# A batched matrix product on one core: the first two batches of y are issued from ScalarE's DMA queue

## The chip, the core and the metric

The kernel runs on one core of a Trainium2 chip. A core has five engines that run their own instruction streams and wait for each other through semaphores: TensorE (PE in the profile, with its weight loads as PEld), VectorE (DVE), ScalarE (ACT), GpSimd (POOL) and SyncE (SP). Transfers between HBM and the on-chip memory SBUF are issued as instructions by one of these engines; the profile shows an issue as a row of the issuer's sequencer (SPq for SyncE) and the transfer itself as work of the core's 16 DMA engines. The metric is the device time of one execution in microseconds (us), and the kernel before and the changed one are compared by it.

## What is computed

Thirty-two independent matrix products in float32, each of a 256x512 matrix by a 512x384 one:

```python
batch, dim_i, dim_j, dim_k = 32, 256, 512, 384
x: (batch, dim_i, dim_j) float32     # 16.8 MB
y: (batch, dim_j, dim_k) float32     # 25.2 MB
np.einsum('bij,bjk->bik', x, y).astype(np.float32)   # 12.6 MB
```

The inputs are 41.94 MB and the output is 12.58 MB, the figures that the profile gives as read and written.

## The kernel before

x is loaded four batches at a time (`Q = 4`), in 8 transfers of 2048 KB. The 128 partitions hold 4 batches of 32 row groups; each partition takes 8 successive rows of x, 16 KB in one piece. y is loaded one batch per transfer (768 KB, 6 KB in one piece per partition), two batches to a tile (`G = 2`), so there are 16 steps, called units u below, and 32 transfers of y. The output of a unit is stored by one transfer of 768 KB, 16 in all. Every transfer is issued by SyncE, in the order in which the program writes them, because each is passed to `keep`, which fixes the order of instructions on their engine.

For every group of four batches, TensorE turns the rows of x over (L99, a transpose against an identity matrix, 32 per group in two halves), and VectorE and ScalarE take turns in copying the result out of PSUM as float16 (L105, L107). The y of a unit is cast to float16 by the two engines in turn (`round_y`, L116 on ScalarE and L118 on VectorE). `multiply(u)` then makes 32 matrix products (L130) into four PSUM tiles, `collect(u)` copies these to SBUF (L143 on ScalarE, L145 on VectorE), and `store(u)` issues the store (L150).

The loop of L160 is written as a software pipeline. At its step s it issues the loads of unit s + 2, collects unit s - 2, multiplies unit s - 1, casts the y of unit s, makes the transposes of the next group of x, and stores unit s - 2. Before the loop, units 0 and 1 are loaded. So SyncE's order begins with the first group of x (L66), the two batches of y of unit 0 (L81), the second group of x, two batches of unit 1 and two of unit 2; then the third group of x, and so on, with a store between the loads from step 2 on. A store that waits for `collect` holds up what is written behind it on SyncE.

The framework inserts all waits. The pools give three tiles to x, five to y, two each to the float16 copies, five to the output, and four PSUM tiles each to transposes and products. ScalarE's stream begins with the load of its function table, which needs no data; its first copy (L107) needs the fifth to eighth transposes.

Of the kernel before, what the change touches and what calls it, by code (L numbers as in the profile page):

```python
# [1 line left out]

# [5 lines left out]


MM_DT = mybir.dt.float16  # L10
F32 = mybir.dt.float32
P = 128


Q = 4
G = 2

LAG = 4


@with_exitstack
def kernel(
    ctx: ExitStack,
    tc: tile.TileContext,
    x: bass.AP,
    y: bass.AP,
    out: bass.AP,
):
    nc = tc.nc

    B, I, J = x.shape
    _, _, K = y.shape


    M = P // G
    NE = I // M
    NJ = J // P

    PQ = P // Q
    R = I // PQ
    H = R // NE
    U = B // G

    const_pool = ctx.enter_context(tc.tile_pool(name="const", bufs=1))
    x_pool = ctx.enter_context(tc.tile_pool(name="x_pool", bufs=3))
    y_pool = ctx.enter_context(tc.tile_pool(name="y_pool", bufs=5))
    yr_pool = ctx.enter_context(tc.tile_pool(name="yr_pool", bufs=2))
    xt_pool = ctx.enter_context(tc.tile_pool(name="xt_pool", bufs=2))  # L50
    o_pool = ctx.enter_context(tc.tile_pool(name="o_pool", bufs=5))
    tpsum_pool = ctx.enter_context(tc.tile_pool(name="tpsum", bufs=4, space=bass.MemoryType.PSUM))
    opsum_pool = ctx.enter_context(tc.tile_pool(name="opsum", bufs=4, space=bass.MemoryType.PSUM))


    keep = tc.keep_in_program_order

    identity = const_pool.tile([P, P], F32)
    make_identity(nc, identity)

    x_of, y_of, yr_of, xt_of, ps_of, o_of = {}, {}, {}, {}, {}, {}

    def load_x(q):
        x_of[q] = x_pool.tile([P, R, J], F32, name="x_sb")
        keep(
            nc.sync.dma_start(  # L66
                out=x_of[q],
                in_=x[q * Q : (q + 1) * Q].rearrange("g (p r) j -> (g p) r j", r=R),
            )
        )  # L70

    def load(u):

        if u == 0:
            load_x(0)
        if (u + 1) * G % Q == 0 and u + 1 < U:
            load_x((u + 1) * G // Q)
        y_of[u] = y_pool.tile([P, G, NJ, K], F32, name="y_sb")
        for g in range(G):
            keep(  # L80
                nc.sync.dma_start(  # L81
                    out=y_of[u][:, g],
                    in_=y[u * G + g].rearrange("(q t) k -> q t k", q=P),
                )
            )

    def transpose(q, half):

        x_sb = x_of[q]
        if half == 0:  # L90
            xt_of[q] = xt_pool.tile([P, NJ, NE, Q * PQ, H], MM_DT, name="xt_sb")
        n = 0
        for t in range(half * NJ // 2, (half + 1) * NJ // 2):
            for e in range(0, NE, 2):
                t_ps = tpsum_pool.tile([P, 2, H, Q * PQ], F32, name="t_ps")
                for f in range(2):
                    for h in range(H):
                        keep(
                            nc.tensor.transpose(  # L99
                                t_ps[:, f, h], x_sb[:, h * NE + e + f, t::NJ], identity  # L100
                            )
                        )
                dst = xt_of[q][:, t, e : e + 2].rearrange("c f p h -> c f h p")
                if n % 2 == 0:
                    keep(nc.vector.tensor_copy(dst, t_ps))  # L105
                else:
                    keep(nc.scalar.copy(dst, t_ps))  # L107
                n += 1

    def round_y(u):  # L110
        y_sb = y_of.pop(u)
        yr_of[u] = yr_pool.tile([P, G, NJ, K], MM_DT, name="y_r")
        for g in range(G):
            for t in range(NJ):
                if t % 2 == 0:
                    keep(nc.scalar.copy(yr_of[u][:, g, t], y_sb[:, g, t]))  # L116
                else:
                    keep(nc.vector.tensor_copy(yr_of[u][:, g, t], y_sb[:, g, t]))  # L118

    def multiply(u):  # L120
        xt_sb, y_r = xt_of[u * G // Q], yr_of.pop(u)
        ps_of[u] = []
        for e in range(NE):
            o_ps = opsum_pool.tile([P, K], F32, name="o_ps")
            ps_of[u].append(o_ps)
            for t in range(NJ):
                for g in range(G):
                    a = (u * G + g) % Q
                    keep(
                        nc.tensor.matmul(  # L130
                            o_ps[g * M : (g + 1) * M],
                            xt_sb[:, t, e, a * PQ : (a + 1) * PQ].rearrange("c p h -> c (p h)"),
                            y_r[:, g, t],
                            start=(t == 0),
                            stop=(t == NJ - 1),
                        )
                    )

    def collect(u):
        o_of[u] = o_pool.tile([P, NE, K], F32, name="o_sb")  # L140
        for e in range(NE):
            if e % 2 == 0:
                keep(nc.scalar.copy(o_of[u][:, e], ps_of[u][e]))  # L143
            else:
                keep(nc.vector.tensor_copy(o_of[u][:, e], ps_of[u][e]))  # L145
        del ps_of[u]

    def store(u):
        keep(
            nc.sync.dma_start(  # L150
                out=out[u * G : (u + 1) * G].rearrange("g (m e) k -> (g m) e k", e=NE),
                in_=o_of.pop(u),
            )
        )


    ahead = LAG - 2
    for u in range(ahead):
        load(u)
    for s in range(U + 2):  # L160
        if s + ahead < U:
            load(s + ahead)
        if s == 0:
            transpose(0, 0)
            transpose(0, 1)
        if s >= 2:
            collect(s - 2)
        if 1 <= s <= U:
            multiply(s - 1)
        if s < U:  # L170
            round_y(s)
        for half in range(2):
            q = (s + 1 - half) * G // Q
            if (s + 1 - half) * G % Q == 0 and 0 < q < B // Q:
                transpose(q, half)
        if s >= 2:
            store(s - 2)


# [1 line left out]
_INS = ['x', 'y']  # L181
_OUTS = [((32, 256, 384), 'float32')]


# [23 lines left out]
```

## Time and profile before

| what | value |
|---|---|
| median of 5 runs | 136.11 us (136.0 to 136.46) |
| the profiled execution | 136.0 us, of which the span of the profile is 134.1 us |
| TensorE busy | 89.6 us (67%) |
| VectorE, ScalarE busy | 56.2 us (42%), 63.9 us (48%) |
| the DMA queue's packets, as a share of 16 engines' span | 97.9% |
| transfers | 56, together 54.53 MB |
| mean rate over the span | 406 GB/s read and written |

The span runs from the first instruction to the last of the profiled execution; 1.9 us of the time lie outside it. The views used are the page (shares by engine, 40 slices, queues, the chain of work that ended last, groups of instructions), the instructions in order of time, the waits, and tables of short stretches. In a row of the order of time, the first number is the start in us from the span's start, the second the time to the end of the last instruction of the merged row, and brackets give the idle time before it and what ended it. In a table of stretches the columns are the stretch, its length, the busy time of PE, PEld, DVE, ACT and POOL with instruction counts, the granted TensorE clock, the share of the DMA engines' time, and GB/s; bytes count where their packet starts, so a share can pass 1.

### The profile page before, as it was taken

What the parts mean: (1) busy time and instruction counts of PE and PEld (TensorE: products, weight loads), DVE (VectorE), ACT (ScalarE), POOL (GpSimd) and SP (SyncE); (2) the same over time, 40 slices, a digit from 0 to 9 for tenths busy, and PEclk for the clock granted to TensorE, in tenths of its full rate; (3) what the DMA queues carried; (4) which work ended last, traced back from release to release, by engine and by line L of the source; (5) the groups of instructions that cost most, each with busy time, mean ns of one, the idle gap of its engine ahead of it and who ended that gap; (6) DMA issues with size and microseconds to landing.
All of it is one profiled execution on the core that took longest, in us unless ns stands there. A gap on an engine that the chain in (4) does not pass through costs nothing.

```text
span 134.1 us, 1968 instructions
## 1 busy us (share of the span) xinstructions
PE 89.6 (67%) x768; PEld 73.9 (55%) x768; DVE 56.2 (42%) x128; ACT 63.9 (48%) x129; POOL 0.7 (1%) x6
## 2 busy tenths in 40 slices
PE   0049494979189786886089780997839792597920
PEld 0049474868168665666068660776727682476810
DVE  0004617471652456611634418324273704628520
ACT  3004837661771467621754428424375605737710
POOL 2000000000000000000000000000000000000000
PEclk9999999999959999999968996579977999779998
DMA  5999999999999999999999999999999999999993
GB/s 107 415 398 462 398 431 412 450 404 410 416 451 415 408 425 423 452 398 421 415 448 431 403 421 421 451 423 399 423 425 453 406 412 420 427 421 423 419 394 164
DMA packets 8074, 54.65 MB, mean 407 GB/s; under 512 B 897, under 2 KB 897, under 8 KB 7041
## 3 DMA queue, kind: packets, MB, share of 16 engines
q1 hardware_dynamic: 8064, 54.53, 97.9%
q8 instruction: 6, 0.10, 0.3%
q14 instruction: 4, 0.02, 0.0%
HBM read 41.94 MB, written 12.58 MB: 406 GB/s over the span
## 4 chain that ended last, share of the span: by engine, by line
DMA 78%; PE 13%; ACT 4%; DVE 0%; issue 0%
DMA y_sb<-in_y_dram 40%; DMA x_sb<-in_x_dram 38%; PE o_ps L130 9%; PE t_ps L99 3%; ACT xt_sb L107 2%; ACT y_r L116 1%; ACT o_sb L143 1%; DVE o_sb L145 0%
## 5 line engine op out<-in xcount | busy, mean ns | idle before, releaser
L130 PE MATMUL o_ps<-y_r,xt_sb 128*64 128x384 f16 x512 | 53.6, 370 | 28.9 <-ACT o_sb L143 21.1
L130 PEld LDWEIGHTS <-xt_sb 128*64 128x64 f16 x512 | 39.9, 124 | 39.7 <-issue 22.8
L116 ACT CAST y_r<-y_sb 128x384 f16<-128x384 f32 x64 | 29.5, 513 | 37.7 <-DMA y_sb<-in_y_dram 37.6
L99 PE MATMUL t_ps<-identity,x_sb 128*128 128x128 f32 x256 | 36.8, 301 | 10.0 <-DMA x_sb<-in_x_dram 9.9
L99 PEld LDWEIGHTS t_ps<-identity,x_sb 128*128 128x128 f32 x256 | 34.0, 211 | 14.5 <-issue 14.1
L118 DVE CAST y_r<-y_sb 128x384 f16<-128x384 f32 x64 | 20.0, 356 | 45.6 <-DMA y_sb<-in_y_dram 45.6
L107 ACT CAST xt_sb<-t_ps 128x512 f16<-128x512 f32 x32 | 22.5, 731 | 24.7 <-PE t_ps L99 24.6
L105 DVE CAST xt_sb<-t_ps 128x512 f16<-128x512 f32 x32 | 22.5, 728 | 25.0 <-PE t_ps L99 24.9
L145 DVE COPY o_sb<-o_ps 128x384 f32<-128x384 f32 x32 | 16.3, 545 | 2.1 <-PE o_ps L130 2.1
L143 ACT COPY o_sb<-o_ps 128x384 f32<-128x384 f32 x32 | 13.9, 492 | 1.3 <-PE o_ps L130 1.3
L107 ACT ACT_TABLE_LOAD x1 | 1.3, 1283 | 0.7 <-PEq L192 0.7
masks.py:199 POOL TENSOR_SCALAR_AFFINE_SELECT identity<-identity 128x128 f32<-128x128 f32 x1 | 0.3, 292 | 0.1
masks.py:197 POOL MEMSET identity<- 128x128 f32 x1 | 0.2, 204 | 0.3 <-POOLq L192 0.3
L192 POOL MEMSET const-bfloat16-1.0<- 128x1 bf16 x1 | 0.1, 101 | 0.0
L192 POOL MEMSET const-uint8-127<- 128x1 uint8 x1 | 0.1, 101 | 0.0
L192 POOL MEMSET const-float32-0.0<- 128x1 f32 x1 | 0.1, 98 | 0.2 <-issue 0.2
L192 POOL MEMSET const-float32-1.0<- 128x1 f32 x1 | 0.1, 98 | 0.0
## 6 DMA issues: line engine op xcount, KB each, us to landing
y_sb<-in_y_dram SPq DMA_DIRECT2D x32, 768.0 KB, 17.9
x_sb<-in_x_dram SPq DMA_DIRECT2D x8, 2048.0 KB, 20.8
out_dram<-o_sb SPq DMA_DIRECT2D x16, 768.0 KB, 17.8
```

The costliest lines, as they stand in the source:

```text
L99: nc.tensor.transpose(t_ps[:, f, h], x_sb[:, h * NE + e + f, t::NJ], identity)
L105: keep(nc.vector.tensor_copy(dst, t_ps))
L107: keep(nc.scalar.copy(dst, t_ps))
L116: keep(nc.scalar.copy(yr_of[u][:, g, t], y_sb[:, g, t]))
L118: keep(nc.vector.tensor_copy(yr_of[u][:, g, t], y_sb[:, g, t]))
L130: nc.tensor.matmul(o_ps[g * M : (g + 1) * M], xt_sb[:, t, e, a * PQ : (a + 1) * PQ].rearrange("c p h -> c (p h)"), y_r[:, g, t], start=(t ...
L143: keep(nc.scalar.copy(o_of[u][:, e], ps_of[u][e]))
L145: keep(nc.vector.tensor_copy(o_of[u][:, e], ps_of[u][e]))
L192: nc = _bacc.Bacc("TRN2", target_bir_lowering=False, num_devices=1)
```

## The change

In `load`, the two y transfers of unit 0 are issued by ScalarE instead of SyncE. All other transfers stay on SyncE, in their order. On SyncE the second group of x thereby follows directly on the first. On ScalarE the two issues are the first instructions that the program writes for this engine. No tile, pool, size or computation changes.

```diff
         y_of[u] = y_pool.tile([P, G, NJ, K], F32, name="y_sb")
         for g in range(G):
+
+            queue = nc.scalar if u == 0 else nc.sync
             keep(
-                nc.sync.dma_start(
+                queue.dma_start(
                     out=y_of[u][:, g],
                     in_=y[u * G + g].rearrange("(q t) k -> q t k", q=P),
                 )
```

## The prediction

> **What bounds the kernel now.** I read the page first: the shares, the 40 slices, the queues and the chain.
>
> ```profile
> span 134.1 us, 1968 instructions
> PE 89.6 (67%) x768; PEld 73.9 (55%) x768; DVE 56.2 (42%) x128; ACT 63.9 (48%) x129; POOL 0.7 (1%) x6
> DMA  5999999999999999999999999999999999999993
> DMA packets 8074, 54.65 MB, mean 407 GB/s; under 512 B 897, under 2 KB 897, under 8 KB 7041
> q1 hardware_dynamic: 8064, 54.53, 97.9%
> DMA 78%; PE 13%; ACT 4%; DVE 0%; issue 0%
> ```
>
> The reader is to see that no compute engine passes 67%, that the DMA digit is 9 in 38 of 40 slices, and that 78% of the chain is DMA. The kernel is one long stream of 54.53 MB through 16 DMA engines, and its time is when that stream starts, how fast it runs and how long the work after it is. An edit that neither takes bytes away nor moves the stream's two ends can only act through its rate.
>
> Second, the start, in order of time, for who issues and who waits there.
>
> ```profile
> 0.73 1.28 ACT L107 ACT_TABLE_LOAD   x1 [0.73 <-PEq L192]
> 0.74 0.37 SPq L66 DMA_DIRECT2D x_sb<-in_x_dram  x1
> 1.16 0.89 SPq L81 DMA_DIRECT2D y_sb<-in_y_dram  x2
> 2.10 0.60 SPq L66 DMA_DIRECT2D x_sb<-in_x_dram  x1
> 2.74 2.02 SPq L81 DMA_DIRECT2D y_sb<-in_y_dram  x4
> 8.49 0.33 SPq L66 DMA_DIRECT2D x_sb<-in_x_dram  x1
> 8.61 6.14 PE L99 MATMUL t_ps<-identity,x_sb 128*128 128x128 f32 x32 [8.61 <-DMA x_sb<-in_x_dram]
> 10.60 0.74 ACT L107 CAST xt_sb<-t_ps 128x512 f16<-128x512 f32 x1 [8.59 <-PE t_ps L99]
> ...
> 23.84 0.35 SPq L150 DMA_DIRECT2D out_dram<-o_sb  x1
> ...
> 32.97 0.93 ACT L116 CAST y_r<-y_sb 128x384 f16<-128x384 f32 x2 [3.07 <-DMA y_sb<-in_y_dram]
> 32.99 0.63 DVE L118 CAST y_r<-y_sb 128x384 f16<-128x384 f32 x2 [3.40 <-DMA y_sb<-in_y_dram]
> 34.78 0.93 ACT L116 CAST y_r<-y_sb 128x384 f16<-128x384 f32 x2 [0.89 <-DMA y_sb<-in_y_dram]
> ```
>
> Eight transfers are issued by 4.76; the ninth (8.49) goes out when the first has landed (8.48). From then on a transfer is issued when the one eight places before it lands. Until 8.61 nothing computes. By 33 us the compute engines have caught up and stand idle for 3.07 and 3.40 us waiting for y.
>
> Third, short stretches at the two ends, for what the stream loses there.
>
> ```profile
> 1.00:2.00 1.00, 0.00 (x0) 0.00 (x0) 0.00 (x0) 1.00 (x1) 0.29 (x1) 1.00 1.11 197
> 2.00:3.00 1.00, 0.00 (x0) 0.00 (x0) 0.00 (x0) 0.01 (x1) 0.00 (x0) 1.00 0.57 131
> 3.00:4.00 1.00, 0.00 (x0) 0.00 (x0) 0.00 (x0) 0.00 (x0) 0.00 (x0) 1.00 0.66 262
> 4.00:5.00 1.00, 0.00 (x0) 0.00 (x0) 0.00 (x0) 0.00 (x0) 0.00 (x0) 1.00 1.05 442
> ...
> 128.00:129.00 1.00, 0.41 (x6) 0.03 (x1) 0.56 (x1) 0.27 (x1) 0.00 (x0) 1.00 1.01 424
> 129.00:130.00 1.00, 0.00 (x0) 0.00 (x0) 0.00 (x1) 0.00 (x0) 0.00 (x0) 1.00 0.83 344
> ```
>
> The last column shows a slow ramp: 131 and 262 GB/s between 2 and 4 us against about 430 after. That is 393 KB where 860 KB could have gone, a loss of 1.1 us of the stream. At the other end the share falls to 0.83 at 129, as the last store is issued: there the stream waits for compute, by about 0.2 us.
>
> **The change, part by part.** First, SyncE loses two issues (0.89 us for both). The first group of x is ahead of them, at 0.74, and stays there. The second group's issue moves from 2.10 to about 1.16, and the four issues behind it, done at 4.76, are done at about 3.8. None of these transfers could have started then: they stand behind 2.1 MB of x that takes until 8.48. Worth 0. The ninth issue waits for the first group's landing, not for SyncE.
>
> Second, ScalarE gains two issues. An issue on SyncE takes 0.33 to 0.60 us in these rows; on ScalarE no row shows it, so I bound it by these: 0.66 to 1.2 us, and take 0.9. Its stream has the table load (1.28 us) and then is idle until 10.60, with 8.59 us of idle time before that first copy. If the issues stand first, the table load ends at about 2.9; if the table load stands first, the issues end at 2.9. Either is 7 us early. Worth 0; without that idle time it would cost the 0.9. Nothing else is queued on ScalarE before the first copy, and the issues wait for nothing, because the tile is fresh.
>
> Third, what moves: the y of unit 0 no longer stands behind the first group of x but beside it. The engines are shared, so the first group of x gets later. A pair of y transfers takes 2 x 786 KB, at 410 GB/s (the 768 KB steps in the waits of ScalarE, such as 32.97 to 34.78, are 1.8 to 1.9 us each) 3.8 us. So the first group of x lands between 8.48 (y gets nothing before x is through) and 12.3 (both y are in first). I take the middle, 10.4, 1.9 us later: one y transfer slips in beside x. On the same sum the second y lands together with the second group of x at about 17.3, since 5.77 MB have then gone in either order, and from unit 1's y on (19.07 in the trace) every landing is where it was.
>
> The Trainium skill, page "DMA: Bandwidth & Descriptors", section "Queues, rings and completion order", says that each DMA engine goes round its queues packet by packet; by it the 128 pieces of 16 KB of x would alternate with the 128 pieces of 6 KB of one y, and x would land at 10.4. No row here has two data queues to show it.
>
> Fourth, who is late when x is late. The 32 transposes (6.14 us) run 10.5 to 16.7 instead of 8.61 to 14.75. The casts of unit 0's y stand behind the copies on both engines and move from 14.93 and 15.38 to 16.8 and 17.3; the second batch, cast about 1 us after the first, is in by 17.3, so it adds nothing. Multiply, collect and the first store move by the same 1.9 us, the store from 23.84 to 25.7. Behind that store on SyncE stand the fourth group of x and two transfers of y. They are late too, but the queue is full: at 23.84 one y of unit 2, the third group of x and the four y of units 3 and 4 are in flight, and the cast of the last of these waits for it until 38.51. A store issued at 25.7, or at 27.6 in the 12.3 case, has over 10 us of transfers in front of it. The lag of 1.9 us ends at 32.97, where ScalarE has 3.07 us and VectorE 3.40 us of idle time waiting for y. In the 12.3 case 3.8 us less 3.07 leaves 0.7, and the next wait (0.89 at 34.78) takes that. Worth 0. Without those idle times the lag would have to be paid at the last store, at most 3.8 us.
>
> Fifth, the rate, the only thing left. For some 15 us two queues feed the engines, which no row shows. On the good side the second queue could put packets where the ramp has holes: at most the 1.1 us above. On the bad side, the nearest row for mixed traffic is the page's slices in which loads run beside stores: the lowest before the tail is 398 GB/s, against a mean of 422, 5.7%; over 13.6 us (3.7 to 17.3) that is 0.8 us. Between -1.1 and +0.8 I take 0: with one queue the engines' share is 1.0 after 4 us on loads alone, about 425 GB/s, so nothing is left to fill there, and the slices with stores have a mean within 1% of that, so mixing as such shows no price.
>
> The rule that speaks against the change is on the same page, section "Issuing engines are not separate DMA queues": transfers started by different engines run on the same 16 DMA engines, and a second issuer saves only issue time. By it the sum is the 0.89 us of SyncE, hidden as said, so 0; by the holes in the ramp it would be up to -1.1. The ramp's rows show a share of 0.57 and 0.66, so they don't settle it.
>
> The sum is 0+0+0+0+0 against the profiled execution: span 134.1 plus 1.9 outside it gives 136.0. That execution is 0.11 below the median of the runs shown, 136.11; no change is therefore forecast as 136.1.
>
> **The rivals.**
>
> A, faster: the second queue fills the ramp. For it: shares of 0.57 and 0.66 between 2 and 4 us while seven more transfers stood issued or were being issued, so the engines had work and did not take it. [...] Half of the 1.1 gives 135.6, all of it 135.0. It counts as faster once a quarter (0.27 us) is regained.
>
> B, slower: in the first 17 us the mixed streams run slower, at the price of the 398 GB/s slice: 136.1 + 0.8 = 136.9, half of it 136.5. For it: two inputs far apart in memory, in pieces of 16 and 6 KB. Against: the mean of 422 beside stores. It decides from a loss of 2% of the rate over 13.6 us, 0.27 us.
>
> C, slower: the lag reaches the last store. For it: at 129 the stream waits for compute, so any lag left there counts in full. Against: the 3.07 and 0.89 us above, and waits for y of 0.8 us and more at nearly every unit after. It needs a lag above 4 us, that is x landing after 12.5; 1 us left over would give 137.1.
>
> D, the change doesn't do what it says: the table load stands first on ScalarE, y is issued at 2.0, and x has the ramp to itself. Then x lands nearer 8.48, and the time is 136.1 as in the main case.
>
> **How the numbers follow.** A measurement of this kernel tells about 0.2% (0.27 us) from no change. No change, with D in it: 0.38. A: 0.33. B: 0.22, C with any other disturbance of the tail 0.07. The likeliest gives 136.1, its own range 135.8 to 136.4. For 8 in 10 the range goes to most of A (135.3) and of B (136.9); 0.1 is left out on either side. Faster 0.33, same 0.38, slower 0.29.
>
> **What would show it.** A second data queue carrying 1.57 MB; the first transposes at 10.5 rather than 8.6, the first store at 25.7; unit 1's y cast at 19.07 as before; the waits for y at about 33 shorter by 1.9 us; from 40 us on every issue within 0.2 us of where it was. If A holds, the table of stretches has more than 200 GB/s at 2 to 3 us, and all landings from unit 1 on shift earlier by one amount; if B, later by one amount, with slices 2 to 5 below 400 on the mean. If the shift appears first in the last 20 us, I am wrong about the tail.

## The result, and the profile after

The changed kernel takes 136.43 us (median of 32 runs, 135.82 to 137.01) where the kernel before takes 136.06 us (54 runs, 135.86 to 136.55). The ratio is 1.0023, with a 95% interval of 1.0016 to 1.0030. That is 0.3 us slower: little, but clear of no change. No change was the forecast. The runs of the changed kernel also spread wider.

The page of the kernel after: shares, DMA, queues, and the chain by engine.

```profile
span 134.4 us, 1968 instructions
PE 91.0 (68%) x768; PEld 74.3 (55%) x768; DVE 56.6 (42%) x128; ACT 64.1 (48%) x129; POOL 0.7 (1%) x6
DMA  4999999999999999999999999999999999999993
q1 hardware_dynamic: 7776, 52.96, 94.6%
q10 hardware_dynamic: 288, 1.57, 3.0%
DMA 83%; PE 9%; ACT 2%; SPq 1%; DVE 0%; issue 0%
```

The second data queue is there (q10, 1.57 MB, the two batches of y). The rest of the page looks much as before: DMA bounds the kernel, no compute engine passes 68%.

The order of time of the kernel after, over the same places as the rows shown of before:

```profile
0.73 0.89 ACTq L83 DMA_DIRECT2D y_sb<-in_y_dram  x2
0.74 0.85 SPq L66 DMA_DIRECT2D x_sb<-in_x_dram  x2
1.65 1.28 ACT L109 ACT_TABLE_LOAD   x1 [1.65 <-PEq L194]
10.50 6.59 PE L101 MATMUL t_ps<-identity,x_sb 128*128 128x128 f32 x32 [10.50 <-DMA x_sb<-in_x_dram]
...
19.05 0.63 DVE L120 CAST y_r<-y_sb 128x384 f16<-128x384 f32 x2 [0.62 <-DMA y_sb<-in_y_dram]
...
25.60 0.35 SPq L152 DMA_DIRECT2D out_dram<-o_sb  x1
...
32.43 0.92 ACT L118 CAST y_r<-y_sb 128x384 f16<-128x384 f32 x2 [0.80 <-DMA y_sb<-in_y_dram]
...
34.23 0.93 ACT L118 CAST y_r<-y_sb 128x384 f16<-128x384 f32 x2 [0.88 <-DMA y_sb<-in_y_dram]
...
38.74 0.92 ACT L118 CAST y_r<-y_sb 128x384 f16<-128x384 f32 x2 [0.50 <-DMA y_sb<-in_y_dram]
...
104.71 5.18 SPq L83 DMA_DIRECT2D y_sb<-in_y_dram  x2
```

Three rows of the kernel before to set beside them:

```profile
19.07 0.92 ACT L116 CAST y_r<-y_sb 128x384 f16<-128x384 f32 x2 [1.96 <-DMA y_sb<-in_y_dram]
38.51 0.63 DVE L118 CAST y_r<-y_sb 128x384 f16<-128x384 f32 x2 [0.43 <-DMA y_sb<-in_y_dram]
104.43 5.22 SPq L81 DMA_DIRECT2D y_sb<-in_y_dram  x2
```

The transposes start at 10.50, unit 1's y is cast at 19.05 (19.07 before), and unit 3's y is even early: 32.43 and 34.23, where before has 32.97 and 34.78. Then comes the place that matters. The second y of unit 4 is waited for until 38.74; before, it was 38.51. Between 34.23 and 38.74 the stream goes from half a microsecond early to a quarter late, and it stays so: SyncE's issue at 104.71 was at 104.43. The work after the last load starts at the same time in both profiles (the last copy at 128.44 before and 128.47 after). So in this pair of traces the loss has one place, 34 to 38 us, long after the second queue's last landing at 17.3.

Four microseconds of that place, in the table of stretches of the kernel before and then of the kernel after (last column GB/s):

```profile
33.00:37.00 4.00, 1.18 (x10) 1.09 (x10) 2.84 (x8) 3.11 (x7) 0.00 (x0) 1.00 1.02 419
```

```profile
33.00:37.00 4.00, 2.94 (x26) 2.50 (x23) 2.84 (x7) 2.96 (x7) 0.00 (x0) 1.00 1.02 410
```

The share of DMA time is 1.02 in both, yet fewer bytes pass: the packets take longer. The trace holds a record of every DMA packet. A 6 KB packet of y takes 234 ns nearly always. Between 33 and 37 us the kernel after has four of over 300 ns (334, 547, 426 and 968 ns); the kernel before has one (364 ns).

Why one engine is enough: each transfer has a share on all 16 DMA engines and has landed when the last of them is through. The trace's semaphore records give the 16 times of every transfer. The last time of unit 4's second y is 38.49 in the kernel before and 38.72 in the kernel after, and the casts that wait for it start 0.02 us later, at 38.51 and 38.74. In the kernel after, the last engine is through with unit 4's first y at 36.10 and needs 2.62 us for the second, where each of the others needs at most 2.0. The packet of 968 ns starts at 36.09, and what it takes beyond 234 ns, 0.73 us, is what this engine falls further behind the middle one (from 1.48 to 2.21 us).

For unit 2's second y the times are, first, middle and last engine:

```
                 first    middle   last
before           24.01    24.33    24.69 us
after            23.91    24.08    24.69
after_again      23.64    23.97    24.61
```

The start did regain something: the middle engine is 0.25 us ahead. At this point the last engine has gained nothing, and only it counts. The half microsecond of gain at 32 us comes behind it. At 27.1 us in the kernel before and 28.9 in the kernel after, a 16 KB fetch of instructions (queue q8) falls on one DMA engine: one of the 16 times of the transfers behind it jumps back, to 1.77 us behind the middle one before and to 1.48 after, and that engine is the last from then on. So of 0.54 us, 0.25 are the middle engine's gain, and 0.29 are how far back that engine falls, which differs from run to run (about 1.2 us in a second trace of the kernel before).

### The profile page after: what moved, and what is told of

Same layout as the page of the kernel before. It is cut to its first block, busy times and chain, and to the rows that moved or that the text cites. A ratio compares the mean times of both kernels' runs of the same rounds, so it can differ in the third digit from the quotient of the medians.

```text
span 134.4 us, 1968 instructions
## 1 busy us (share of the span) xinstructions
PE 91.0 (68%) x768; PEld 74.3 (55%) x768; DVE 56.6 (42%) x128; ACT 64.1 (48%) x129; POOL 0.7 (1%) x6
## 3 DMA queue, kind: packets, MB, share of 16 engines
q10 hardware_dynamic: 288, 1.57, 3.0%
## 4 chain that ended last, share of the span: by engine, by line
DMA 83%; PE 9%; ACT 2%; SPq 1%; DVE 0%; issue 0%
DMA y_sb<-in_y_dram 54%; DMA x_sb<-in_x_dram 15%; DMA out_dram<-o_sb 13%; PE o_ps L132 7%; PE t_ps L101 2%; ACT xt_sb L109 1%; ACT y_r L118 1%; SPq L66 1%; DVE o_sb L147 0%; ACT o_sb L145 0%; SPq L152 0%
## 5 line engine op out<-in xcount | busy, mean ns | idle before, releaser
L132 PE MATMUL o_ps<-y_r,xt_sb 128*64 128x384 f16 x512 | 54.6, 374 | 26.9 <-ACT o_sb L145 19.2
L101 PE MATMUL t_ps<-identity,x_sb 128*128 128x128 f32 x256 | 37.3, 304 | 10.5 <-DMA x_sb<-in_x_dram 10.5
L101 PEld LDWEIGHTS t_ps<-identity,x_sb 128*128 128x128 f32 x256 | 34.5, 212 | 15.6 <-issue 15.6
```

The lines of the kernel that those rows point to most:

```text
L101: nc.tensor.transpose(t_ps[:, f, h], x_sb[:, h * NE + e + f, t::NJ], identity)
L132: nc.tensor.matmul(o_ps[g * M : (g + 1) * M], xt_sb[:, t, e, a * PQ : (a + 1) * PQ].rearrange("c p h -> c (p h)"), y_r[:, g, t], start=(t ...
```

## The experiments

Beside the times, two stretches of each trace are compared: 1 to 4 us (how fast the stream starts) and 33 to 37 us (the place of the loss). What stands at that place in SyncE's queue, in the kernel before and in the changed one, are unit 4's two y (through on the middle engine at 34.86 and 36.74 in the kernel before), and behind them the first store. The stretch from 1 to 4 us in the kernel before, then in the kernel after:

```profile
1.00:4.00 3.00, 0.00 (x0) 0.00 (x0) 0.00 (x0) 1.01 (x1) 0.29 (x1) 1.00 0.78 197
```

```profile
1.00:4.00 3.00, 0.00 (x0) 0.00 (x0) 0.00 (x0) 1.28 (x1) 0.29 (x1) 1.00 0.71 201
```

**The changed kernel and the kernel before, once more.** No edit.

> The changed kernel once more, for a second trace of it. Theory 1 (rings): with two queues at the start the 16 DMA engines drift apart, and the slowest of them ends the run; then the trace shows again a last landing that is later, against the middle one of the 16 engines, than in the kernel before (2.3 us against 2.1 from first to last), and the time is again 1.002 of before. Theory 2 (late compute): x lands 2 us later, everything computed starts 2 us later, and some of that reaches the end; the same time of 1.002, but the landings of the y transfers need not be late. If the 0.28 us that the first trace gains between 34 and 39 us is chance, the new trace has it elsewhere or not at all.

> The kernel before once more, for a second trace: fewer than five y packets above 300 ns between 32 and 39 us, as in its first trace, and 136.1, if the slow packets belong to the changed order of the start; some twenty if they come and go by chance.

Measured: after_again 136.52 us, 1.0024 (1.0009 to 1.0038); before_again 135.93 us in one run. The same two stretches of after_again, then of before_again:

```profile
1.00:4.00 3.00, 0.00 (x0) 0.00 (x0) 0.00 (x0) 1.28 (x1) 0.29 (x1) 1.00 0.72 216
33.00:37.00 4.00, 2.87 (x26) 2.44 (x23) 2.84 (x7) 3.08 (x8) 0.00 (x0) 1.00 1.01 386
```

```profile
1.00:4.00 3.00, 0.00 (x0) 0.00 (x0) 0.00 (x0) 1.02 (x1) 0.29 (x1) 1.00 0.76 186
33.00:37.00 4.00, 2.22 (x19) 2.11 (x21) 2.85 (x8) 3.12 (x8) 0.00 (x0) 1.00 1.02 419
```

The slow place is there again, stronger: 386 GB/s, 22 slow y packets, and SyncE's issue of 104.71 stands at 105.06. The last engine's lag behind the middle one grows over unit 4's two y from 1.69 to 2.69 us. In the kernel before the place is missing again (419 GB/s, one slow packet, a lag of 1.25 and 1.22 us). How strong it is varies from run to run, which fits the wider spread of the changed kernel's times.

**Late compute, without touching the transfers.**

```diff
-                for f in range(2):
-                    for h in range(H):
+                for f, h in [(f, h) for f in range(2) for h in range(H)] * (2 if q == 0 and t == 0 else 1):
```

> The kernel before with 16 of the first group's transposes made twice (the same result is written again), so that compute starts late by about 2 to 4 us while all transfers stay on one queue in their old order. Theory 1 (rings): 1.000, 136.05. Theory 2 (late compute): 1.002, 136.4.

The edit makes eight transposes twice, not the sixteen that the expectation names, and the first store is issued at 24.90 instead of 23.84. Measured: 136.12 us, 1.0001 (0.9987 to 1.0016), 415 GB/s at 33 to 37 us. A lag of 1.1 us costs nothing; larger ones come below.

**x late on one queue, and half of the change.** In x_between the first group of x is issued by SyncE between the two y of unit 0, and ScalarE issues nothing. In act_y0a only the first y is on ScalarE.

```diff
-        if u == 0:
-            load_x(0)
...
         for g in range(G):
+            if u == 0 and g == 1:
+                load_x(0)
             keep(
                 nc.sync.dma_start(
```

```diff
-            queue = nc.scalar if u == 0 else nc.sync
+            queue = nc.scalar if u == 0 and g == 0 else nc.sync
```

> The kernel before with the first y transfer issued ahead of the first group of x, all on one queue: x lands at about 10.4 as in the changed kernel, without a second queue. Theory 1 (rings): 1.000, 136.05. Theory 2 (late compute): 1.002, 136.4.

> Only the first y transfer is issued by ScalarE, the second stays on SyncE behind x. x lands at 10.4 as in the changed kernel, and the second queue is in use for 7 us instead of 13. Theory 1 (rings), if the price grows with the time of two queues: half of it, 1.001; if it comes from the start alone: 1.002. Theory 2 (late compute): 1.002, since x is as late.

Measured: x_between 136.85 us, 1.0046 (1.0029 to 1.0064); act_y0a 136.53 us, 1.0022 (1.0006 to 1.0037). The stretches of x_between:

```profile
1.00:4.00 3.00, 0.00 (x0) 0.00 (x0) 0.00 (x0) 1.01 (x1) 0.29 (x1) 1.00 0.84 317
33.00:37.00 4.00, 1.97 (x19) 1.86 (x19) 2.83 (x7) 3.11 (x7) 0.00 (x0) 1.00 0.99 306
```

act_y0a costs about as much as the whole change, with 393 GB/s and 16 slow packets at 33 to 37 us, though its interval holds half the price too. The theory that the price needs two queues falls: in x_between one queue alone makes the loss twice as large. x_between starts far faster than before (317 GB/s against 197) and is far slower at 33 to 37 us (306 against 419; 61 slow packets). What it won at the start it pays there, and more.

**What the place is.** shift10 delays all of x_between's transfers by three memsets of the first tile loaded; reversed takes x_between's batches from the end.

```diff
+        if u == 0:
+            for _ in range(3):
+                keep(nc.vector.memset(y_of[u], 0.0))
```

```diff
+    def place(u):
+        per = Q // G
+        return (B // Q - 1 - u // per) * per + u % per
...
-                in_=x[q * Q : (q + 1) * Q].rearrange(
+                in_=x[(B // Q - 1 - q) * Q : (B // Q - q) * Q].rearrange(
...
-                    in_=y[u * G + g].rearrange("(q t) k -> q t k", q=P),
+                    in_=y[place(u) * G + g].rearrange("(q t) k -> q t k", q=P),
```

(The store's address in reversed follows in the same way.)

> The kernel x_between, whose trace has its slow y packets (300 to 1400 ns instead of 234) between 33.4 and 36.7 us, with three memsets of unit 0's y tile ahead of the first load, so that all transfers start some 8 to 10 us later. Theory 3 (place in the stream: the 16 engines, left closely in step by the start, collide when the last y of units 3 and 4 are read): the slow packets move with the stream, to about 42 to 46 us. Theory 4 (an event of the chip at a fixed time): they stay at 33 to 37 us. The time is that of x_between plus the delay, about 145 to 147 us.

> The kernel x_between with the batches taken from the end: other addresses of x, y and the output at every place of the stream, the same tiles and the same order. If the slow packets belong to the addresses read (the tenth batch of y), they are gone from 33 to 37 us, and the time falls below 136.8, to before's 136.1 or, as the start of x_between moves more bytes, to 135.6. If they belong to the place in the stream or to the tiles written: still there, 136.8.

Measured: shift10 146.4 us in one run, with the loads 10 us later; its slow packets lie between 43.8 and 46.7 us (two more, near 39 us, follow a fetch of instructions), 10 us later too. The event is not tied to the clock but to the stream. reversed 136.68 us, 1.0044 (1.0028 to 1.0060), 338 GB/s at 33 to 37 us: other addresses, the same loss. One microsecond of shift10 at a time:

```profile
43.00:44.00 1.00, 1.00 (x11) 1.00 (x10) 0.23 (x1) 0.23 (x1) 0.00 (x0) 1.00 1.09 418
44.00:45.00 1.00, 0.44 (x4) 0.35 (x4) 1.00 (x4) 1.00 (x3) 0.00 (x0) 1.00 0.94 270
45.00:46.00 1.00, 0.00 (x0) 0.00 (x0) 1.00 (x4) 1.00 (x3) 0.00 (x0) 1.00 0.98 233
```

**The first store, or the last of the five y tiles.** store_later is x_between with `LAG = 5`; six_y is x_between with `bufs=6` in y_pool.

```diff
-LAG = 4
+LAG = 5
```

```diff
-    y_pool = ctx.enter_context(tc.tile_pool(name="y_pool", bufs=5))
+    y_pool = ctx.enter_context(tc.tile_pool(name="y_pool", bufs=6))
```

> The kernel x_between with loads issued one step earlier (LAG = 5), so that the first store stands behind the fourth group of x and unit 5's y, not behind unit 4's; the order of the loads themselves is unchanged. Theory 5 (the stream's first store disturbs the y packets just ahead of it): no slow packets at 33 to 37 us, instead at about 42 to 46 us, ahead of the first store in its new place. Theory 6 (the tile or the place of unit 4's second y): they stay at 33 to 37 us. Time by either theory between 136.0 and 136.8.

> The kernel x_between with six y tiles in place of five, so that unit 4's y is no longer the last tile used for the first time and the addresses behind the y pool shift by 12 KB. Theory 5 (first store): slow packets stay at 33 to 37 us, 136.8. Theory 6 (the last y tile's first use): they move to unit 5's y at 42 to 46 us.

Measured: store_later 136.61 us, 1.0038 (1.0023 to 1.0053); six_y 137.24 us, 1.0075 (1.0047 to 1.0102, four runs), 313 GB/s at 33 to 37 us. store_later at the old place and at the new one:

```profile
33.00:37.00 4.00, 2.06 (x21) 1.90 (x22) 3.05 (x8) 3.12 (x8) 0.00 (x0) 1.00 1.07 444
43.00:44.00 1.00, 0.13 (x3) 0.11 (x4) 1.00 (x3) 0.91 (x2) 0.00 (x0) 1.00 1.14 289
44.00:45.00 1.00, 1.00 (x14) 0.86 (x15) 0.24 (x1) 0.55 (x2) 0.00 (x0) 1.00 0.87 313
```

The slow y packets have left the old place and stand at 42.7 to 45.4 us, again just ahead of the first store in SyncE's queue. With six tiles they stay. So the place goes with the first store, not with a tile.

**A small store ahead of all.** Both kernels with 64 KB of the identity stored to a corner of the output that the real store later writes over.

```diff
     for u in range(ahead):
         load(u)
+        if u == 0:
+            keep(nc.sync.dma_start(out=out[0, :P, :P], in_=identity))
```

> The changed kernel with a small store of 64 KB (the identity, to a corner of the output that the first real store writes over) issued by SyncE right after the first group of x. Theory 5 (the stream's first store disturbs the loads ahead of it, and the start decides how much): the disturbance moves to the start, no slow y packets at 34 to 37 us, and the time falls from 1.0023 to between 0.998 and 1.001, the 0.15 us of the small store included. If it is not being the first store that matters but any store among loads at that place, the slow packets stay and the time is 1.002 to 1.003.

> The kernel x_between with the same small store right after unit 0's second y. Theory 5: no slow packets at 33 to 37 us, and the 0.99 us per engine that they cost there is gone or moved to the start: 0.997 to 1.001 in place of 1.0046. Otherwise: the slow packets stay, 1.004 to 1.006.

Measured: after_early 136.68 us, 1.0037 (1.0022 to 1.0052), 384 GB/s at 33 to 37 us; x_between_early 137.31 us, 1.0071 (1.0048 to 1.0095). The slow packets stay where they were. That it is the first write of the run is not the reason, then; the first full store's place in a stream of loads is what the runs show, and no more.

**The start.** Three edits ask whether the start decides how much that place costs. y0_after_ramp puts a memset and two dummy copies ahead of ScalarE's issues, so that y is issued at 4.01. y0_after_x puts a small copy there that reads the first group of x, so that y is issued at 8.59, when x has landed. x_halves is the kernel before, one queue, x first, with only the first group of x cut into two transfers.

```diff
+            if u == 0 and g == 0:
+                pad = const_pool.tile([P, 2, 1536], F32, name="pad")
+                keep(nc.vector.memset(pad[:, 0], 0.0))
+                for _ in range(2):
+                    keep(nc.scalar.copy(pad[:, 1], pad[:, 0]))
```

```diff
+            if u == 0 and g == 0:
+                pad = const_pool.tile([P, 8], F32, name="pad")
+                keep(nc.scalar.copy(pad, x_of[0][:, 0, :8]))
```

```diff
+        whole = x[q * Q : (q + 1) * Q].rearrange("g (p r) j -> (g p) r j", r=R)
+        parts = 2 if q == 0 else 1
+        for k in range(parts):
+            rows = slice(k * R // parts, (k + 1) * R // parts)
+            keep(nc.sync.dma_start(out=x_of[q][:, rows], in_=whole[:, rows]))
```

> The changed kernel with two dummy copies on ScalarE ahead of its two issues, so that y begins some 3 to 5 us later and the slow first packets are x's alone, as in the kernel before; the second queue and the late x remain. Theory 3 (the start sets how closely the engines are in step): few or no slow packets at 34 to 37 us, 1.000 to 1.001. If order or the second queue as such costs: 1.002 to 1.003, with the slow packets.

> The changed kernel with a small copy on ScalarE that reads the first group of x ahead of its two issues, so that y starts when x has landed: the start is that of before, the second queue works beside the second group of x. Theory 7: 0.999 to 1.001, under five slow y packets at 34 to 37 us. If the second queue costs wherever it runs: 1.002.

> The kernel before, one queue and x first, with the first group of x issued as two transfers of half its rows, pieces of 8 KB in place of 16. Theory 7 (how the first packets start the 16 engines decides how much the first store's place costs): less is lost to slow packets before 5 us than the 0.97 us per engine of before, slow y packets appear at 34 to 37 us, and the time is 1.001 to 1.004. Theory 8 (only y beside or ahead of x does it, by the order): no slow packets at 34 to 37 us, 0.997 to 1.000.

Measured: y0_after_ramp 136.17 us, 1.0006 (0.9991 to 1.0021); y0_after_x 136.14 us, 1.0002 (0.9989 to 1.0015); x_halves 136.75 us, 1.0046 (1.0027 to 1.0066). The stretches of y0_after_x, then of x_halves:

```profile
1.00:4.00 3.00, 0.00 (x0) 0.00 (x0) 0.00 (x0) 1.01 (x1) 0.29 (x1) 1.00 0.75 197
33.00:37.00 4.00, 3.14 (x37) 2.67 (x37) 2.76 (x8) 3.64 (x8) 0.00 (x0) 1.00 1.01 413
```

```profile
1.00:4.00 3.00, 0.00 (x0) 0.00 (x0) 0.00 (x0) 1.01 (x1) 0.29 (x1) 1.00 0.73 224
33.00:37.00 4.00, 1.49 (x14) 1.30 (x14) 2.87 (x7) 3.13 (x8) 0.00 (x0) 0.90 1.02 373
```

These two are the pair that decides. y0_after_x keeps the start of before (197 GB/s) and has the second queue, beside the second group of x; its first store is issued at 29.46, later than the 25.60 of the changed kernel. It costs nothing that these runs can tell: neither the second queue nor late compute is the reason. x_halves has one queue, the old order and early compute, and differs in the first pieces; it costs twice what the change does, with 31 slow packets at the old place. One reserve: x_halves has one transfer more than before, so that each issue from the ninth on follows a transfer one place further on; x_between does not have that and shows the same.

The rate of the stretch is from one execution each, the ratio from all runs, and one trace can hold other accidents: that of y0_after_x is an execution of 136.33 us, whose issues get 0.4 us late between 64.92 and 67.22, with no slow stretch at 33 to 37 us.

y0_after_ramp lies between: x has the first packets to itself, ten slow packets remain, and its interval holds both no change and most of the change's 1.0023. Its trace is of its slowest execution (136.95 us).

**The first store on the other queue.**

```diff
+        queue = nc.scalar if u == 0 else nc.sync
         keep(
-            nc.sync.dma_start(
+            queue.dma_start(
                 out=out[u * G : (u + 1) * G].rearrange("g (m e) k -> (g m) e k", e=NE),
```

> The kernel x_between with unit 0's store issued by ScalarE, so that it goes beside the loads on a queue of its own from about 29 us, not behind unit 4's y on SyncE's. If the 0.99 us per engine at 33 to 37 us come from the place where one queue passes from loads to its first store, they are gone or small and the time falls from 1.0046 to 0.996 to 1.000. If the store's being there at all costs: 1.003 to 1.006, slow packets moved to 29 to 33 us or to the second store's place (43 to 47 us).

> The same with the changed kernel. If the passage from loads to the first store on one queue is the cause: from 1.0023 to 0.998 to 1.001. Otherwise 1.002 or more.

Measured: x_between_store_act 136.62 us, 1.0031 (1.0013 to 1.0048); after_store_act 136.20 us, 1.0013 (0.9997 to 1.0028). Each is lower than the kernel that it comes from, but the intervals overlap, so that a gain is likely and not shown. In after_store_act the store is issued at 29.03, and the slow packets move to 31.5 to 33 us: they go with the store here too. The expectation that they vanish was wrong.

The readings side by side, for the kernels whose first full store stands at the old place. The third column is what had landed early: bytes of packets that ended before 5 us. The one before the last is the time that the last of the 16 engines needs for unit 4's two y.

| kernel | GB/s, 1 to 4 us | MB by 5 us | GB/s, 33 to 37 us | y packets over 300 ns there | last engine, unit 4's y, us | ratio to before |
|---|---|---|---|---|---|---|
| before | 197 | 0.77 | 419 | 1 | 3.73 | 1 |
| y0_after_x | 197 | 0.77 | 413 | 4 | 3.72 | 1.0002 |
| pe_late | 202 | 0.75 | 415 | 3 | 3.90 | 1.0001 |
| y0_after_ramp | 224 | 0.79 | 404 | 10 | 4.14 | 1.0006 |
| after | 201 | 0.88 | 410 | 4 | 4.51 | 1.0023 |
| act_y0a | 220 | 0.92 | 393 | 16 | 4.67 | 1.0022 |
| after_again | 216 | 0.98 | 386 | 22 | 4.83 | 1.0024 |
| after_early | 210 | 0.96 | 384 | 24 | 4.87 | 1.0037 |
| x_halves | 224 | 0.95 | 373 | 31 | 4.87 | 1.0046 |
| reversed | 321 | 1.00 | 338 | 37 | 5.14 | 1.0044 |
| six_y | 284 | 1.00 | 313 | 62 | 5.39 | 1.0075 |
| x_between | 317 | 1.00 | 306 | 61 | 5.56 | 1.0046 |
| x_between_early | 294 | 1.00 | 323 | 53 | 5.59 | 1.0071 |

The last engine's time at that place orders the ratios nearly throughout. The GB/s from 1 to 4 us alone do not order them, since they count a packet's bytes where it starts: y0_after_ramp has the 224 of x_halves, but much less of it had landed by 5 us. Of the four slow packets of y0_after_x, the first two (33.4 to 34.4 us) follow its fetch of instructions at 32.4.

## Why the prediction was wrong

The forecast was 136.1 us, and the measured 136.43 lies within the range given, but it is a small loss and not no change. Point by point, by its own steps:

*What bounds the kernel* was right. Every difference found is one of the DMA stream's rate, and no engine's work.

*SyncE's two issues, worth 0:* right. The second group of x is issued at once behind the first, and nothing starts earlier by it.

*ScalarE's two issues, worth 0, taken as 0.9 us:* right. They take 0.89 us and stand ahead of the table load, which ends at 2.93; the first copy there comes at 12.49.

*x later by 1.9 us:* right. The first transposes start at 10.50 (10.5 was given), and unit 1's y is cast at 19.05. The Trainium skill's "DMA: Bandwidth & Descriptors", section "Queues, rings and completion order", has each DMA engine go round its queues packet by packet, but a packet there is typically 9 to 17 descriptors; the prediction took every 16 KB and 6 KB piece for one. Here the turns did go piece by piece: x landed at 10.37 and unit 0's first y at 10.53, as they would with one 6 KB piece of y beside each 16 KB piece of x. Had a queue kept its turn for all eight pieces that a transfer has on an engine, one of the two would have been through long before the other.

*The lag ends by 33 us, worth 0:* right. The first store is issued at 25.60 (25.7 was given), ScalarE's idle time at the wait for unit 3's y shrinks from 3.07 to 0.80 us, and pe_late and y0_after_x, with lags of 1.1 us and of 5.6 us at the first store, cost nothing measurable.

*The rate, "the only thing left", taken as 0 between -1.1 and +0.8:* this is the step that failed. It looked for a price only where two queues feed the engines, up to 17.3 us. There the change gains: slices 2 to 5 of the page have a mean of 427 GB/s after and 418 before, and the middle engine is 0.25 us ahead by 24 us. The price stands 17 us later, just ahead of the first store, where the last engine of the traced run loses 0.78 us against the kernel before (4.51 in place of 3.73); what it had gained until then was 0.54. How large the price is goes by how the stream began. Nothing in the trace of before pointed there, because the same place costs nothing after that kernel's own start. The sum also took the stream as one thing, when each landing waits for the last of 16 engines. That the measured time is only 0.3 us from the forecast was luck: the gain before that place and the loss at it nearly cancel.

Of the rivals, B (slower, from mixed streams in the first 17 us) had the sign and the rough size (+0.3 of at most 0.8) but not the place: its own sign, slices 2 to 5 below 400, is contradicted. A (the ramp filled) happened in part and was paid back. C and D did not happen: the lag is gone by 33 us, and y was issued at 0.73, ahead of the table load. The test "from 40 us on every issue within 0.2 us of where it was" caught it: the shift is 0.22 to 0.29 us at every issue from 40 us to 111 us.

The rule that spoke against the change, from the same page's section "Issuing engines are not separate DMA queues", says that a second issuer saves only issue time. These runs agree: y0_after_x, with the second queue and the old start, is at 1.0002 (0.9989 to 1.0015). That the order and the piece sizes of the first loads can cost something 30 us later is shown by the runs alone.

What stays open is the mechanism. The runs show that the slow packets stand where the first full store meets the loads, that they go with that store, and that the kernels in which more had landed by 5 us have more of them. Why engines that start more quickly should collide there, whether in HBM, in SBUF or on the way, no run here tells. A start that keeps the gain without paying later was not found.

## What to carry to other kernels

In a kernel bound by one long DMA stream, the order of the first transfers is not free even when the compute engines make up the lag that it gives them: changing it, or only the size of the first pieces, cost up to 0.46% here, at a place 30 us further on. Look for such a loss by comparing the landings of the same transfer in both traces until they part, then at the rate of that stretch. And reckon with the last of the DMA engines, not the mean: at 24 us most engines of the changed kernel were ahead, and no landing was.

## What the runs showed of the hardware

- The first packets of a run are slow. A 16 KB packet takes 611 ns in steady work, but the first 16 of the kernel before take 0.7 to 1.85 us. Starting with 6 KB packets instead (x_between) moves 317 GB/s between 1 and 4 us in place of 197, and 1.00 MB in place of 0.77 had landed by 5 us.
- Where the first full store meets loads, y packets of 234 ns can take 300 to 1475 ns for some 3 us, at a share of DMA time of about 1 (0.99 in x_between, at 306 GB/s; 1.02 in before, at 419). The share says nothing of this; the GB/s column does. One packet of 968 ns on the last engine was enough to make the changed kernel's traced run late.
- A fetch of instructions goes through the same DMA engines. At 27.1 us in the kernel before, a 16 KB fetch (queue q8) took 1060 ns, and an x packet that starts as it ends 1114 in place of 611. Before it the last engine was 0.36 us behind the middle one, after it 1.77 us. Where the kernel's first such fetch falls differs from run to run: 25.5 us in pe_late, 32.4 in y0_after_x.
